# First feed-forward output by seven products for six block pairs, modulation spread over both mixers' outputs, last right-half products deferred

## The chip, the cores and the metric

The kernel runs on one NeuronCore of one Trainium2 chip. The time is microseconds on the device for one execution. TensorE is called PE in the profile, VectorE DVE, ScalarE ACT, GpSimd POOL and SyncE SP; each takes its instructions strictly in the order in which they stand in its queue, and the queues wait for each other by semaphores. Transfers between the device's memory and the on-chip buffers are issued by SP for the most part.

## What is computed

One step of a two-layer diffusion backbone over 640 tokens (512 latent, 128 context) of width 1024, in float32. Layer 0 mixes tokens by latent attention and neighbourhood attention, layer 1 by grouped-query attention; after each stands a SwiGLU feed-forward. Shift, scale and gate of every sub-layer come from a modulation vector; the two token groups have different ones.

```python
def ada_modulation(cond, w_mod, b_mod):
    m = jax.nn.silu(cond) @ w_mod + b_mod
    return jnp.split(m, 6, axis=-1)

def swiglu(h, w_in, w_out):
    gate, up = jnp.split(h @ w_in, 2, axis=-1)
    return (jax.nn.silu(gate) * up) @ w_out

for l in range(DEPTH):
    ...
    xs = xs + g1_s * out_s
    hs = modulate(rms_norm(xs, norm_ffn[l]), sh2_s, sc2_s)
    xs = xs + g2_s * swiglu(hs, w_ffn_in[l], w_ffn_out[l])
```

The hidden width of the feed-forward is 2816, which is 22 blocks of 128.

## The kernel before

Activations lie transposed: eight tiles `x[0]` to `x[7]` of 128 features by 640 tokens. A product works on a half of 320 tokens, left (c = 0) or right (c = 1); the right half holds 192 latent and 128 context tokens, so its evacuation with the gate (`residual`, L319 to L323) takes two DVE instructions where the left takes one. Every float32 factor is split into a high part, written by ACT, and a low part, written by DVE (in some places POOL) as the difference; a product of two split factors is three 128x320 products on PE (`mm3`, recorded at L63).

*Modulation.* The modulation of layer 0 for the first sub-layers is computed at the start. The remaining 56 tiles (eight for the gate G2 of layer 0, eight for each of the six parts of layer 1) are made on the side. One such tile is a load of 512 KB into `wm` and two DVE instructions `junk<-wm,cb`, which multiply it by the activated condition `cb` and sum along the row into `mods`. `mod_side` builds a function `step` that the feed-forward calls; its `plan` says how many tiles are fetched at which call. Before, 17 tiles were made in layer 0's feed-forward loop (one in each of the blocks 5 to 21), 11 in the first pass of its output, 20 in the second pass, and the last 8 in layer 1's loop.

*Mixer output* (`mixer_out`, tiles named `oa` in layer 0, `oc` in layer 1). Eight output tiles n. For n = 0 to 4 both halves are computed and evacuated at once; for 5, 6 and 7 the left halves come first, then PE runs `oanp` or `ocnp`, the product with ones that sums the squares for the norm of the left half, between right-half products of 5, 6, 7. The squares are made by ACT and added up by DVE into `oanacc` or `ocnacc` (L215), so the norm's product needs the last addition. The weights `oaw`, `ocw` of tile n are split by DVE for even n and by POOL for odd n (L185). After the norm, DVE makes the inputs of the feed-forward (`h01`, `h11`).

*Feed-forward* (`ffn`). A loop over the 22 hidden blocks computes gate and up by seven products for eight; the hidden blocks are split and most are spilled to memory. In layer 1 (`paired`), blocks 7 to 18 form six pairs (`PAIRS`); `split_pair` makes sums and differences of the two blocks and halves there (`T1` to `T4`, `B11`, `B21`, `B22`), so that the output product of a pair for two output tiles takes seven products instead of eight.

*Feed-forward output, first pass.* For each output tile n the blocks in `FIRST` (nine in layer 0, ten in layer 1) are multiplied, evacuated, and written back to `x[n]`. *Second pass.* In layer 0 the remaining 13 blocks are multiplied plainly, in 8 output tiles (names `fo_1_na`), with the last two tiles' right halves held back until the norm of the left half is under way. In layer 1 the second pass goes by pairs of output tiles p = 0 to 3 with seven products each, in the order S2, A11, S3, A12, A22, S1, S4 (`PLAN`): the weights S1, S2, S3, S4 are sums and differences of the raw blocks A11, A12, A21, A22, made by DVE (L1675 to L1685) and split at L1692 and L1693 three places ahead of their use. Their raw loads go through a ring of three buffers, tag `raw`, which the modulation tiles of the feed-forward's output use too.

## Time and profile before

Three runs took 1478.83, 1478.95 and 1480.19 us; the median is 1478.95. The profiled execution took 1480.2 us, of which the span from the first to the last instruction is 1478.4.

| stage | from, us | to, us |
|---|---|---|
| layer 0 mixer output (`oa`) | 303 | 377 |
| layer 0 feed-forward loop | 413 | 653 |
| layer 0 output, first pass | 654 | 717 |
| layer 0 output, second pass | 717 | 808 |
| layer 1 attention | 808 | 973 |
| layer 1 mixer output (`oc`) | 973 | 1045 |
| layer 1 feed-forward loop | 1082 | 1321 |
| layer 1 output, first pass | 1321 | 1391 |
| layer 1 output, second pass | 1391 | 1466 |
| last norm and stores | 1466 | 1478 |

A row of the timeline gives start, duration, engine, line, operation, output tile and input tiles, shape, and in brackets how long the engine was idle ahead of it and what released it. The name of a tile is its program name without buffer numbers. A row of busy time by stretch gives, for each engine, busy microseconds and the number of instructions, then the TensorE clock that was granted (1.00 is full), the DMA engines' share and the rate in GB/s.

### The profile page before, as it was taken

How to read it: one execution, taken by the hardware profiler on the slowest of the kernel's cores; microseconds unless marked ns; L12 is line 12 of the kernel's file. 1: busy time of each engine (PE TensorE's matmuls, PEld its weight loads, DVE VectorE, ACT ScalarE, POOL GpSimd, SP SyncE). 2: the span in 40 equal slices, each digit the busy share in tenths (PEclk: the TensorE clock that was granted, in tenths of full speed). 3: DMA queues.
4: the chain of work that ended last, by engine and by line, in shares of the span. 5: the costliest groups of instructions: out<-in, count | busy, mean ns of one | idle time of the engine just before them, and what ended most of it. 6: DMA issues, size and time to landing. Idle time of an engine off the chain costs nothing.

```text
span 1478.4 us, 25725 instructions
## 1 busy us (share of the span) xinstructions
PE 1440.5 (97%) x9785; PEld 1391.9 (94%) x9785; DVE 1202.6 (81%) x2236; ACT 769.9 (52%) x1521; POOL 210.9 (14%) x302
## 2 busy tenths in 40 slices
PE   5999999999999999999999999999999999999997
...
DVE  5686688876989999967997888766999999954496
...
GB/s 372 219 152 142 178 67 37 29 55 189 30 204 190 189 184 182 168 229 336 271 217 114 95 55 31 29 44 123 29 196 169 190 197 209 207 224 303 196 86 72
DMA packets 80651, 229.53 MB, mean 155 GB/s; under 512 B 9136, under 2 KB 14736, under 8 KB 80144
## 3 DMA queue, kind: packets, MB, share of 16 engines
...
## 4 chain that ended last, share of the span: by engine, by line
PE 85%; DVE 6%; ACT 4%; DMA 2%; issue 2%; SPq 0%; POOL 0%; DVEq 0%; ACTq 0%; POOLq 0%
PE fg L63 21%; PE fd L63 10%; PE fo L63 8%; PE fu L63 6%; PE gq L63 3%; DMA mraw<-in_wm 2%; PE nk L63 2%; PE nq L63 2%; PE fo_2b L63 1%; PE fo_0b L63 1%; PE gs L63 1%; PE fo_2a L63 1%; PE fo_0a L63 1%; PE go L63 1%; PE fo_4b L63 1%
## 5 line engine op out<-in xcount | busy, mean ns | idle before, releaser
L1805 DVE SCALAR_TENSOR_TENSOR junk<-wm,cb 128x1024 bf16<-128x1024 f32 x62 | 75.7, 1221 | 5.4 <-DMA wm<-in_wm 4.7
L1248 ACT ACTIVATE sg<-g 128x320 f32<-128x320 f32 x34 | 16.0, 472 | 115.0 <-DVE g L1248 115.0
L63 PE MATMUL gq<-h10h,wgq 128*128 128x320 f32 x256 | 66.7, 318 | 0.0
L255 POOL TENSOR_SCALAR h10h<-h10t,gs,mods 128x320 fp32r<-128x320 f32 x4 | 3.6, 888 | 429.5 <-DVE h10t L249 427.8
L1248 DVE SCALAR_TENSOR_TENSOR junk<-wm,cb 128x1024 bf16<-128x1024 f32 x50 | 61.1, 1221 | 0.8
L1248 DVE TENSOR_TENSOR wY<-s,wY 128x1024 fp32r<-128x1024 f32 x40 | 48.8, 1220 | 2.2 <-ACT wY L1248 2.2
L1248 DVE TENSOR_TENSOR wZ<-s,wZ 128x1024 fp32r<-128x1024 f32 x40 | 48.8, 1220 | 0.0
L63 PEld LDWEIGHTS gq<-h10h,wgq 128*128 128x128 f32 x256 | 45.0, 188 | 0.9 <-PE gtp L67 0.2
L1248 ACT ACTIVATE wZ<-s 128x1024 fp32r<-128x1024 f32 x40 | 42.4, 1060 | 0.1
L1248 ACT ACTIVATE wY<-s 128x1024 fp32r<-128x1024 f32 x40 | 42.0, 1049 | 0.0
L63 PE MATMUL gq<-h10l,wgq 128*128 128x320 f32 x128 | 39.5, 308 | 0.0
L1987 ACT ACTIVATE gp<-gs,gb,rq 128x640 f32<-128x640 f32 (+1 forms) x40 | 31.9, 797 | 14.5 <-DVE gb L1986 14.1
L63 PE MATMUL fg<-h11E,wW 128*128 128x320 f32 x240 | 38.7, 310 | 0.0
L63 PE MATMUL fg<-h11q,wX 128*128 128x320 f32 x240 | 38.6, 309 | 0.0
L63 PE MATMUL fg<-h01q,wX 128*128 128x320 f32 x240 | 38.6, 309 | 0.0
L63 PE MATMUL fg<-h11N,wZ 128*128 128x320 f32 x240 | 38.6, 309 | 0.0
L63 PE MATMUL fg<-h01N,wZ 128*128 128x320 f32 x240 | 38.6, 309 | 0.0
L63 PE MATMUL fu<-h01q,wX 128*128 128x320 f32 x240 | 38.6, 309 | 0.0
L63 PE MATMUL fu<-h11q,wX 128*128 128x320 f32 x240 | 38.6, 309 | 0.0
L63 PE MATMUL fg<-h01E,wW 128*128 128x320 f32 x240 | 38.6, 309 | 0.0
L63 PE MATMUL fd<-h11q,wZ 128*128 128x320 f32 x240 | 38.5, 309 | 0.0
L63 PE MATMUL fd<-h01q,wZ 128*128 128x320 f32 x240 | 38.5, 309 | 0.0
...
## 6 DMA issues: line engine op xcount, KB each, us to landing
wm<-in_wm SPq DMA_DIRECT2D x48, 512.0 KB, 4.0
mraw<-in_wm SPq DMA_DIRECT2D x8, 1024.0 KB, 15.4
mraw<-in_wm SPq DMA_DIRECT2D x16, 512.0 KB, 3.9
...
mrow<-in_wm0g POOLq DMA_DIRECT2D x8, 512.0 KB, 6.4
wm<-in_wm0g SPq DMA_DIRECT2D x8, 512.0 KB, 3.5
...
```

Of the source, the lines that this page charges most:

```text
L63: cls.last = nc.tensor.matmul(*a, **k)
L255: G.tensor_scalar(h[:, c0:c1], t, self.gsl[:, k, 0:1], self.ml[:, self.sh + k, 0:1], ALU.mult, ALU.add)
L1248: self.last = after(self.last, lambda: op(*a, **k))
L1805: def step(kind, at, line=lambda op, *a, **k: op(*a, **k)):
L1987: weighed.append((S.activation(dst, src, AF.Exp, bias=nb, scale=rq[:, j:j + 1], accum_out=ll[:, j:j + 1]), v))
```

## The change

Four things change together.

1. *Layer 0's output goes as layer 1's.* `FO_ORDER` is one list for both layers, `FIRST` has ten blocks in both, `split_pair` runs in layer 0's loop too, and the second pass has seven products for each of four pairs of output tiles.
2. *The second pass has a new order*, for both layers. `PLAN` is now a list of (p, product): for p = 0 and 1 S2, A11, S1, S4, S3, A12, A22; for p = 2 and 3 the left half's products S2, A11, S3, A12, A22; and at the end S1 and S4 of 2 and of 3. The norm of the left half is taken after A22 of p = 3, and the next layer's left inputs (or the final scaling) are made beside the deferred right-half products.
3. *Modulation is spread over both mixers' outputs.* There is one list `left` of 56 tiles; 8 are made in `oa` (1, 2, 2, 2, 1 at n = 0 to 4), 12 in layer 0's loop, 18 in the first pass of its output (1, 2, 2, 2, 2, 3, 3, 3), none in the second pass, 10 in `oc` (two at each n), 8 in layer 1's loop. In the mixers the tiles use a ring of two buffers, in the first pass the `raw` ring of three.
4. `cb` is loaded from the already activated condition `crs`, so its four activations and the input `crow` go.

```diff
-FO_ORDER = (TAIL + list(range(FB - 3)), TAIL + list(range(7)) + list(range(7, FB - 3, 2)) + list(range(8, FB - 3, 2)))
+FO_ORDER = TAIL + list(range(7)) + list(range(7, FB - 3, 2)) + list(range(8, FB - 3, 2))
...
-    def mixer_out(wsrc, os_, order, xin, ml, name, nxt, pre, begun, behind):
+    def mixer_out(wsrc, os_, order, xin, ml, name, nxt, pre, begun, behind, step):
...
                                 evac(i, c, ps[c])
+                            step("o", i)
                         held = []
...
                         evac(n, c, ps[c])
+                    step("o", n)
...
-        paired = l == 1
-        nf = 10 if paired else 9
-        FIRST, SECOND = FO_ORDER[l][:nf], FO_ORDER[l][nf:]
+        FIRST = FO_ORDER[:10]
...
-            PLAN = ("S2", "T2", "b"), ("A11", "B11", "a"), ("S3", "T3", "b"), ("A12", "B21", "a"), ("A22", "T4", "b"), \
-                ("S1", "T1", "c"), ("S4", "B22", "d")
+        KIND = {"S2": ("T2", "b"), "A11": ("B11", "a"), "S3": ("T3", "b"), "A12": ("B21", "a"), "A22": ("T4", "b"),
+                "S1": ("T1", "c"), "S4": ("B22", "d")}
+        LEFT, RIGHT = ("S2", "A11", "S3", "A12", "A22"), ("S1", "S4")
+        PLAN = [(p, c) for p in (0, 1) for c in LEFT[:2] + RIGHT + LEFT[2:]] + [(p, c) for p in (2, 3) for c in LEFT] + \
+            [(p, c) for p in (2, 3) for c in RIGHT]
...
+            if late and c in RIGHT:
+                if l == 1:
+                    scale_final(x, 1, n + 1 if c == "S1" else n)
+                nxt(x, nrm, 0, [next(order), next(order)])
...
-    def mod_side(todo, plan):
+    left = [(l, src[i], j0, i) for l, src, j0 in [(0, wm0g[:8], G2)] + [(1, wm1[j:j + 8], j) for j in (SH1, SC1, G1, SH2, SC2, G2)]
+            for i in range(8)]
+
+    def mod_side(plan):
...
+                    if raws is None:
+                        raw = load(src, D, f"wm{l}_{j0 + i}")
+                    else:
+                        raw = raws.tile([P, D], F32, tag="ws", bufs=2, name=f"wm{l}_{j0 + i}")
+                        nc.sync.dma_start(raw, src)
...
-    x, pend = mixer_out(wOA, oMs + oNs, [4, 5, 6, 7, 0, 1, 2, 3], x_again, mods[0], "oa", nxt, op[-1], begun, scored)
+    x, pend = mixer_out(wOA, oMs + oNs, [4, 5, 6, 7, 0, 1, 2, 3], x_again, mods[0], "oa", nxt, op[-1], begun, scored,
+                        mod_side(lambda kind, i: (1, 2, 2, 2, 1)[i])(op[1], op[5]))
...
-    side = mod_side([(0, wm0g[:8], G2)] + [(1, wm1[j:j + 8], j) for j in (SH1, SC1, G1, SH2, SC2)],
-                    lambda kind, i: int(i > 4) if kind == "fb" else (0, 1, 1, 1, 2, 2, 2, 2, 3, 3, 3, 3, 2, 2, 2, 2)[i])
+    side = mod_side(lambda kind, i: int(i in (5, 6, 7, 8, 10, 12, 14, 16, 18, 19, 20, 21)) if kind == "fb" else
+                    (1, 2, 2, 2, 2, 3, 3, 3)[i])
...
-    x, pend = mixer_out(wOC, oGs, list(range(8)), lambda n, x=x: x[n], mods[1], "oc", nxt, op[-1], begun, None)
+    x, pend = mixer_out(wOC, oGs, list(range(8)), lambda n, x=x: x[n], mods[1], "oc", nxt, op[-1], begun, None,
+                        mod_side(lambda kind, i: (2, 2, 2, 2, 2)[i])(op[1], op[5]))
```

Where the instructions stand now is seen best in DVE's queue. The first place is the start of `oc`, layer 1's mixer output: `xr` and `lead` are the residual tiles, `oc0a` and so on the sums in PSUM, `ocnsq` the squares, `ocw` the weights of the mixer's output. Before:

```order
L323 SCALAR_TENSOR_TENSOR xr_4323<-oc0a,mods_99,xr_4323 128x320
L323 SCALAR_TENSOR_TENSOR xr_4323<-oc0b,mods_99,xr_4323 128x192
L323 SCALAR_TENSOR_TENSOR xr_4323<-oc0b,mods_99,xr_4323 128x128
L323 SCALAR_TENSOR_TENSOR xr_4337<-oc1a,mods_99,xr_4337 128x320
L323 SCALAR_TENSOR_TENSOR xr_4337<-oc1b,mods_99,xr_4337 128x192
L323 SCALAR_TENSOR_TENSOR xr_4337<-oc1b,mods_99,xr_4337 128x128
L215 TENSOR_TENSOR ocnacc<-ocnacc,ocnsq_12077 128x320
L185 TENSOR_TENSOR ocw_12220<-ocw4r,ocw_12220 128x1024
L215 TENSOR_TENSOR ocnacc<-ocnacc,ocnsq_12085 128x320
L323 SCALAR_TENSOR_TENSOR xr_4383<-oc2a,mods_99,xr_4383 128x320
```

In the kernel after the change, from the same evacuation of `oc0a` on:

```order
L323 SCALAR_TENSOR_TENSOR lead_5330<-oc0a,mods_99,lead_5330 128x320
L323 SCALAR_TENSOR_TENSOR lead_5330<-oc0b,mods_99,lead_5330 128x192
L323 SCALAR_TENSOR_TENSOR lead_5330<-oc0b,mods_99,lead_5330 128x128
L1792 SCALAR_TENSOR_TENSOR junk_12227,mods_99<-wm_30_12223,cb 128x1024
L323 SCALAR_TENSOR_TENSOR xr_4344<-oc1a,mods_99,xr_4344 128x320
L1792 SCALAR_TENSOR_TENSOR junk_12229,mods_99<-wm_30_12223,cb 128x1024
L215 TENSOR_TENSOR ocnacc<-ocnacc,ocnsq_12240 128x320
L1792 SCALAR_TENSOR_TENSOR junk_12231,mods_99<-wm_31_12225,cb 128x1024
L323 SCALAR_TENSOR_TENSOR xr_4344<-oc1b,mods_99,xr_4344 128x192
L1792 SCALAR_TENSOR_TENSOR junk_12233,mods_99<-wm_31_12225,cb 128x1024
L323 SCALAR_TENSOR_TENSOR xr_4344<-oc1b,mods_99,xr_4344 128x128
```

The twenty `junk` instructions stand between the evacuations and additions from here on, the last one ahead of the addition for n = 5; the split of `ocw4r`, which was the eighth of these rows, has moved behind the fourteenth `junk`:

```order
L1792 SCALAR_TENSOR_TENSOR junk_12407,mods_99<-wm_36_12403,cb 128x1024
L215 TENSOR_TENSOR ocnacc<-ocnacc,ocnsq_12400 128x320
L1792 SCALAR_TENSOR_TENSOR junk_12409,mods_99<-wm_36_12403,cb 128x1024
L185 TENSOR_TENSOR ocw_12419<-ocw4r,ocw_12419 128x1024
L1792 SCALAR_TENSOR_TENSOR junk_12411,mods_99<-wm_37_12405,cb 128x1024
L323 SCALAR_TENSOR_TENSOR xr_4634<-oc5a,mods_99,xr_4634 128x320
L1792 SCALAR_TENSOR_TENSOR junk_12413,mods_99<-wm_37_12405,cb 128x1024
L185 TENSOR_TENSOR ocw_12532<-ocw6r,ocw_12532 128x1024
L323 SCALAR_TENSOR_TENSOR xr_4560<-oc4a,mods_99,xr_4560 128x320
```

The evacuation of `oc5a` and the split of `ocw6r` now stand ahead of that of `oc4a`.

The second place is DVE's queue at the end of layer 0's first pass (`fo_0_71` is the right half of its last output tile) and the start of its second. After the change:

```order
L1792 SCALAR_TENSOR_TENSOR junk_8813,mods_99<-wm_27_8805,cb 128x1024
L323 SCALAR_TENSOR_TENSOR xr_4710<-fo_0_71_8733,mods_98,xr_4710 128x192
L323 SCALAR_TENSOR_TENSOR xr_4710<-fo_0_71_8733,mods_98,xr_4710 128x128
L1792 SCALAR_TENSOR_TENSOR junk_8815,mods_99<-wm_28_8807,cb 128x1024
L1792 SCALAR_TENSOR_TENSOR junk_8817,mods_99<-wm_28_8807,cb 128x1024
L1792 SCALAR_TENSOR_TENSOR junk_8819,mods_99<-wm_29_8809,cb 128x1024
L1669 TENSOR_TENSOR wo_1_0S_8834<-wo_1_1A21r,wo_1_1A22r 128x768
L1792 SCALAR_TENSOR_TENSOR junk_8821,mods_99<-wm_29_8809,cb 128x1024
L1670 TENSOR_TENSOR wo_1_0S_8835<-wo_1_0S_8834,wo_1_0A11r 128x768
L1691 TENSOR_TENSOR wo_1_0A_8841<-wo_1_0A11r,wo_1_0A_8841 128x768
L1672 TENSOR_TENSOR wo_1_1A21r<-wo_1_0A11r,wo_1_1A21r 128x768
L1691 TENSOR_TENSOR wo_1_0S_8838<-wo_1_0S_8835,wo_1_0S_8838 128x768
```

For comparison the same engine at the same place of layer 1 in the kernel before, where such weights were made already:

```order
L1598 TENSOR_TENSOR wo_0_75_16283<-wo_0_75r,wo_0_75_16283 128x640
L1675 TENSOR_TENSOR wo_1_0S_16373<-wo_1_1A21r,wo_1_1A22r 128x768
L1676 TENSOR_TENSOR wo_1_0S_16374<-wo_1_0S_16373,wo_1_0A11r 128x768
L1678 TENSOR_TENSOR wo_1_1A21r<-wo_1_0A11r,wo_1_1A21r 128x768
L323 SCALAR_TENSOR_TENSOR xr_4622<-fo_0_6a,mods_99,xr_4622 128x320
L1693 TENSOR_TENSOR wo_1_0S_16377<-wo_1_0S_16374,wo_1_0S_16377 128x768
L1693 TENSOR_TENSOR wo_1_0S_16384<-wo_1_1A21r,wo_1_0S_16384 128x768
L323 SCALAR_TENSOR_TENSOR xr_4622<-fo_0_6b,mods_99,xr_4622 128x192
L323 SCALAR_TENSOR_TENSOR xr_4622<-fo_0_6b,mods_99,xr_4622 128x128
L1693 TENSOR_TENSOR wo_1_0A_16380<-wo_1_0A11r,wo_1_0A_16380 128x768
L1681 TENSOR_TENSOR wo_1_0S_16374<-wo_1_0A12r,wo_1_0S_16374 128x768
```

There the sums and splits of `wo_1_0S` stood ahead of the last evacuations of the first pass; in layer 0 of the changed kernel they stand behind the evacuation of `fo_0_71` and among four `junk` instructions.

The third place is the end of a pair of output tiles in layer 1's second pass: the evacuation of p = 0's left half, the additions after A22 (L1748) and the splits of p = 1's S2 (`wo_1_1S_16743`) and S1. After the change:

```order
L215 TENSOR_TENSOR fn1acc<-fn1acc,fn1sq_16768 128x320
L1669 TENSOR_TENSOR wo_1_2S_16739<-wo_1_3A21r,wo_1_3A22r 128x768
L323 SCALAR_TENSOR_TENSOR lead_13211<-fo_1_0a,mods_99,lead_13211 128x320
L1670 TENSOR_TENSOR wo_1_2S_16740<-wo_1_2S_16739,wo_1_2A11r 128x768
L1691 TENSOR_TENSOR wo_1_1A_16771<-wo_1_2A11r,wo_1_1A_16771 128x768
L1748 TENSOR_TENSOR fo_1_0p_16639<-fo_1_0b,fo_1_0p_16639 128x320
L1691 TENSOR_TENSOR wo_1_1S_16743<-wo_1_2S_16740,wo_1_1S_16743 128x768
L1691 TENSOR_TENSOR wo_1_1S_16794<-wo_1_2S_16739,wo_1_1S_16794 128x768
L323 SCALAR_TENSOR_TENSOR xr_4344<-fo_1_0p_16639,mods_99,xr_4344 128x320
```

The split of S2 for the next pair now stands behind the addition that needs A22's product, which is the last product of the pair.

## The prediction

> **What bounds the kernel now.** I read the page first: the busy table, the row of slices and the chain that ended last.

> ```profile
> span 1478.4 us, 25725 instructions
> PE 1440.5 (97%) x9785; PEld 1391.9 (94%) x9785; DVE 1202.6 (81%) x2236; ACT 769.9 (52%) x1521; POOL 210.9 (14%) x302
> PE   5999999999999999999999999999999999999997
> DVE  5686688876989999967997888766999999954496
> PE 85%; DVE 6%; ACT 4%; DMA 2%; issue 2%; SPq 0%; POOL 0%; DVEq 0%; ACTq 0%; POOLq 0%
> ```

> TensorE (PE) is busy in every slice but the first and the last, and the chain runs through it for 85% of the span. So the time is the number of products times their pitch, plus whatever makes PE wait. VectorE (DVE) has 19% free on the whole, but its slices differ: nines in the feed-forward loops, fours and sixes elsewhere. The second view is busy time by stage, with the two mixer stretches on which the argument rests.

> ```profile
> core 0: us, PE busy (x) PEld busy (x) DVE busy (x) ACT busy (x) POOL busy (x), PEclk, DMA share, GB/s
> 413.00:653.00 240.00, 240.00 (x1638) 239.81 (x1637) 223.11 (x325) 120.34 (x198) 0.00 (x0) 1.00 0.56 183
> 653.00:718.00 65.00, 65.00 (x446) 65.00 (x445) 49.97 (x90) 12.19 (x16) 0.00 (x0) 1.00 0.91 327
> 1391.00:1466.00 75.00, 75.00 (x511) 74.57 (x509) 56.84 (x98) 37.04 (x63) 0.00 (x0) 1.00 0.32 110
> 333.20:367.29 34.09, 34.09 (x235) 34.09 (x234) 22.36 (x33) 13.51 (x21) 10.53 (x4) 1.00 0.58 198
> 1001.05:1035.69 34.64, 34.64 (x238) 34.64 (x237) 22.88 (x33) 13.62 (x21) 9.93 (x4) 1.00 0.42 132
> ```

> PE never stops in these stretches. Its pitch is 65.00/446 = 145.7 ns to 75.00/511 = 146.8 ns for one 128x320 product, which is what a product taken away is worth here. DVE has about 12 us free in each mixer stretch.

> **What goes.** Layer 0's first output ran 1056 products; with ten blocks plain (480) and six pairs by seven products (4 x 7 x 18 = 504) it runs 984. The gain is 72 x 0.1465 = **10.5 us**, certain, since PE is full there. Everything else in the change can only give that back: it moves DVE work to places where PE waits for DVE. The unit moved is one modulation tile: one 512 KB load and two DVE products.

> ```profile
> 649.92 1.22 DVE L1248 SCALAR_TENSOR_TENSOR junk<-wm,cb 128x1024 bf16<-128x1024 f32 x1
> 651.07 0.08 DVE L1248 DVE_READ_ACCUMULATOR junk<-wm,cb 128x1 f32 x1
> wm<-in_wm SPq DMA_DIRECT2D x48, 512.0 KB, 4.0
> ```

> One product lasts 1.22 us and holds the queue 1.15 us (649.92 to 651.07); a load lands 4.0 us after its issue.

> **Second mixer (oc): the wait that decides most.** Ten tiles, twenty products, now stand in DVE's queue between the first evacuation of oc and the last addition to its norm, for which PE's ocnp waits in order.

> ```profile
> 1001.05 0.55 DVE L323 SCALAR_TENSOR_TENSOR xr<-oc0a,mods,xr 128x320 f32<-128x320 f32 x1 [5.85 <-PE oc0a L63]
> 1001.52 0.67 DVE L323 SCALAR_TENSOR_TENSOR xr<-oc0b,mods,xr 128x192 f32<-128x192 f32 x2
> 1002.10 0.54 DVE L323 SCALAR_TENSOR_TENSOR xr<-oc1a,mods,xr 128x320 f32<-128x320 f32 x1
> ...
> 1005.31 1.21 DVE L185 TENSOR_TENSOR ocw<-ocw4r,ocw 128x1024 fp32r<-128x1024 f32 x1
> 1006.45 0.48 DVE L215 TENSOR_TENSOR ocnacc<-ocnacc,ocnsq 128x320 f32<-128x320 f32 x1
> 1006.85 0.54 DVE L323 SCALAR_TENSOR_TENSOR xr<-oc2a,mods,xr 128x320 f32<-128x320 f32 x1
> ...
> 1010.86 2.44 DVE L215 TENSOR_TENSOR ocnacc<-ocnacc,ocnsq 128x320 f32<-128x320 f32 x1 [0.78 <-ACT ocnsq L214]
> ...
> 1035.20 0.49 DVE L215 TENSOR_TENSOR ocnacc<-ocnacc,ocnsq 128x320 f32<-128x320 f32 x1 [0.60 <-ACT ocnsq L214]
> 1036.49 0.70 PE L63 MATMUL ocnp<-ocnacc,ones 128*128 128x320 f32 x2
> ```

> The first row starts when PE releases it, so nothing can be done earlier. The queue from there, by starts: 8 left evacuations at 0.47, 5 right ones at 0.58, 11 additions at 0.40, 4 weight splits at 1.14 and three small rows, together 15.9, plus 20 x 1.15 = 23.0: 38.9 us. It ends at 1039.95 at the earliest, against 1035.69. PE would arrive at 1036.49, and 0.44 later because three more right-half products stand ahead, so at least 1039.95 - 1036.93 = 3.0 us are lost (3.8 if the 0.8 from the last addition to ocnp is needed too). Before, some additions were stretched (2.44 instead of 0.48 at 1010.86). By the busy time as it was, 22.88 + 20 x 1.22 = 47.3 us from 1001.05 end at 1048.3, a loss of 11.4. A split of GpSimd's lies under each stretched row, as in the first mixer:

> ```profile
> 342.16 2.42 POOL L185 TENSOR_TENSOR oaw<-oaw5r,oaw 128x1024 fp32r<-128x1024 f32 x1 [5.49 <-ACT oaw L184]
> 342.47 2.45 DVE L215 TENSOR_TENSOR oanacc<-oanacc,oansq 128x320 f32<-128x320 f32 x1 [0.77 <-ACT oansq L214]
> ```

> I expect about half of that stretching to stay: **7 us**, bounds 3.0 and 11.4. [...]

> **First mixer (oa).** Eight tiles, sixteen products.

> ```profile
> 329.24 0.58 DVE L1831 COPY xr<-oMs3l 128x1 f32<-128x1 f32 x8
> 333.20 0.55 DVE L323 SCALAR_TENSOR_TENSOR xr<-oa0a,mods,xr 128x320 f32<-128x320 f32 x1 [3.38 <-PE oa0b L63]
> ...
> 366.80 0.49 DVE L215 TENSOR_TENSOR oanacc<-oanacc,oansq 128x320 f32<-128x320 f32 x1 [0.59 <-ACT oansq L214]
> 368.10 0.70 PE L63 MATMUL oanp<-oanacc,ones 128*128 128x320 f32 x2
> ```

> A product now stands ahead of the first evacuation, so part of the 3.38 us idle serves. Unstretched, 15.7 + 16 x 1.15 = 34.1 us from 329.82 end at 363.9: no loss. By the busy time as it was, 329.82 + 22.36 + 19.5 = 371.7, a loss of 3.6; two buffers for the tiles, with 4.0 us to land, can add 2 more. **3 us**, bounds 0 and 5.6.

> **Start of layer 0's second pass.** In layer 1 of the kernel before, the same weights are made like this:

> ```profile
> 1378.90 0.96 DVE L1675 TENSOR_TENSOR wo_0S<-wo_1A21r,wo_1A22r 128x768 f32<-128x768 f32 x1 [3.22 <-DMA wo_1A22r<-in_wFO]
> 1379.89 0.96 DVE L1676 TENSOR_TENSOR wo_0S<-wo_0S,wo_0A11r 128x768 f32<-128x768 f32 x1
> 1380.88 0.85 ACT L1692 ACTIVATE wo_0S<-wo_0S 128x768 fp32r<-128x768 f32 x1 [6.07 <-DVE wo_0S L1676]
> 1382.10 0.95 DVE L1693 TENSOR_TENSOR wo_0S<-wo_0S,wo_0S 128x768 fp32r<-128x768 f32 x1
> ...
> 1391.67 0.68 DVE L323 SCALAR_TENSOR_TENSOR xr<-fo,mods,xr 128x192 f32<-128x192 f32 x2 [1.65 <-PE fo L63]
> ...
> 1391.47 1.78 PE L63 MATMUL fo_0b<-hr_T,wo_0S 128*128 128x320 f32 x11
> ```

> S2 is split by 1383.05, eight microseconds before PE needs it, and the last evacuation of the first pass comes after. In layer 0 now DVE's queue has that evacuation first, which PE releases only at the pass's end, and behind it three modulation products, the sum S1, a fourth product, S2, the split of A11, a difference and then S2's low half. Counted from PE's last product of the pass: 0.68 + 3 x 1.22 + 0.96 + 1.22 + 0.96 = 7.5, ScalarE's high half 0.85 gives 8.3, and DVE's three rows of 0.95, less an overlap of 0.08 each, give 10.1 for the low half. PE has six products (0.9) to do in between. A11's raw load waits for a buffer that the second product frees and 4.0 us to land, 0.68 + 2.44 + 4.0 = 7.1 against the 6.5 at which S2 could begin: 0.6 more, or 1.4 on a busy queue. **9.5 us**, bounds 8.3 and 11.5, with nothing to hide it: PE's queue is in order.

> **The rest.** Layer 0's first pass gets 18 tiles instead of 11, beside ten blocks of weights: DVE 71.5 us of work by row pitches in about 69 of PE, and 27.5 to 29 MB in that time, some 400 GB/s against the 327 in the row above: 0 to 4, I take 1.2. In both second passes A22 is the last left product, and its row stands ahead of the next pair's S2 split; in layer 1 before, the split ended as follows,

> ```profile
> 1407.61 0.95 DVE L1693 TENSOR_TENSOR wo_1S<-wo_2S,wo_1S 128x768 fp32r<-128x768 f32 x1
> ```

> 1.4 us before the next pair could start (1391.47 + 7 x 18 x 0.1468 = 1409.97), so waits of up to an addition and a split appear at some of three transitions in each layer: 0.3 to 1.5 in each, I take 0.6 and 0.6. Layer 0 also gets a norm product (0.35) and the next layer's left inputs start later in DVE's queue: 0.2 to 2, I take 1.6. At the tail two additions more on the chain, 0.8 by the 0.40 above, less what the earlier left half saves: 0.4. The feed-forward loop of layer 0 loses five tiles (12.2 us of DVE) and gains the operand sums (18.5): about 229 of its 240 us, so one tight block, 0.3, at most 0.7.

> **The clock.** Long waits have a second price here.

> ```profile
> 201.19 0.42 PE L63 MATMUL ns<-nk,nqh 128*128 128x384 f32 x1 [1.05 <-DVE kTl L865]
> 201.90:205.30 3.40, 3.40 (x15) 3.40 (x14) 2.89 (x11) 2.20 (x6) 0.37 (x1) 0.50 0.49 130
> 8.00:12.00 4.00, 0.00 (x0) 0.00 (x0) 3.93 (x13) 3.96 (x11) 0.00 (x0) 1.00 1.03 397
> ```

> After waits of about 1 us, 3.4 us ran at half the granted clock, which is 1.7 us lost; after an empty stretch at 8 to 12 us none did. Three new long waits therefore cost 0 to 5.1; I take 1.7, one window. [...]

> **Sum.** 3 + 7 + 9.5 + 1.2 + 1.2 + 1.6 + 0.4 + 0.3 + 1.7 = 25.9 given back, less 10.5: +15.4 on the profiled execution's 1480.2, which stands 1.25 above the median 1478.95. On the median: **1494**. The bounds add to 12.5 (1481.0) and 44.1 (1512.5).

> **Rivals.**
> *Nothing is stretched.* If GpSimd's splits hold no DVE row up once the queue is packed, oa costs 0 and oc 3.0, no window is halved, and the terms lie at their lower ends: 12.5 - 10.5 = +2.0, 1481.0, within 0.2% of before (1476 to 1482). It decides at the additions: all at 0.49 instead of the 2.44 above. For it: the products leave GpSimd fewer gaps. Against: four splits of 2.4 us are still there. 0.15.
> *The gain stays.* If DVE's queue did not stand between PE and its next weights at the second pass, and the mixers' slack of 12 us covered the twenty products, only 10.5 less some small terms would be seen: 1470 to 1475. It needs DVE to overtake its own queue; 0.05.
> *Saturation.* DMA at 0.91 in the first pass already, now with seven more tiles of 512 KB: if loads land late there, and all three waits halve the clock, 4 + 5.1 instead of 1.2 + 1.7: +21.6, and with oc at its upper end +26.5: 1500 to 1506 and more. 0.17.

> **Numbers.** Forecast 0.63, rivals 0.15, 0.05, 0.17. A measurement of this kernel tells about 0.2% (3 us) from no change. Faster 0.06 (the second rival and a little), same 0.14, slower 0.80. The range 1479 to 1508 leaves out the second rival and the far end of the third.

> **What would show it.** Right: PE idle for 8 to 11 us ahead of layer 0's first S2 product, with S2's low half as releaser; ocnp 4 to 12 us later after its predecessor than before, with the vector engine full from oc0a on; oanp 0 to 6. The first output of layer 0 shows 984 products. Wrong: no gap at the second pass's start, which would mean that S2 was split before the evacuation; or ocnp reached with DVE idle ahead of it.

## The result and the profile after

The changed kernel takes **1515.55 us** (median of 4 runs, 1512.87 to 1518.16); the kernel before, run beside it, takes 1479.57 (4 runs, 1478.83 to 1480.28). The ratio is **1.024, 95% interval 1.0228 to 1.0252**: slower by 36 us. The profiled execution took 1513.64 us with a span of 1511.9, which is 33.5 us more than the span of before. All lengths below are of profiled executions. A wait of PE is given as the time from one product to the next, less one pitch of 0.147 us; the idle time in the bracket of a row is up to 0.3 us shorter.

From the page of the kernel after: the span, the busy table, the slices of PE and of its clock, and the engines' shares of the chain that ended last.

```profile
span 1511.9 us, 25918 instructions
PE 1444.9 (96%) x9715; PEld 1389.6 (92%) x9715; DVE 1255.4 (83%) x2345; ACT 788.0 (52%) x1573; POOL 213.5 (14%) x302
PE   6999999998999999999799999998999999999996
PEclk9999999999999999999899999998999999999998
PE 72%; DVE 14%; DMA 6%; ACT 5%; issue 3%; SPq 0%; DVEq 0%; POOL 0%; ACTq 0%; POOLq 0%
```

PE issues 70 products fewer (72 taken away, 2 for a second norm row), yet its busy time rises by 4.4 us: some of them ran slower. Two slices that were full now show a dip in PE and in the clock, near 740 and near 1040 us; a third, near 360, shows one in PE alone. The chain says who took the time: DVE had 6% of it and has 14%, DMA had 2% and has 6%.

Cut at the same landmarks on PE, the 33.5 us lie as follows (stage lengths, before and after):

| from ... to (on PE) | before | after | difference |
|---|---|---|---|
| start ... first product of oa | 303.12 | 301.73 | -1.4 |
| oa ... oanp, the first mixer's norm | 64.98 | 72.18 | +7.2 |
| oanp ... layer 0's first output product | 282.73 | 284.46 | +1.7 |
| layer 0's output, to its last product | 156.94 | 160.37 | +3.4 (-10.5 of products in it) |
| ... attention's first `gr`, the norm of the queries | 28.46 | 32.67 | +4.2 |
| ... ocnp, the second mixer's norm | 200.26 | 214.52 | +14.3 |
| ocnp ... layer 1's first output product | 282.75 | 284.44 | +1.7 |
| layer 1's output, to the end | 159.15 | 161.49 | +2.3 |

The second mixer first. The windows of the kernel after (columns: length, busy time and count of PE, PEld, DVE, ACT, POOL, then granted clock, DMA share, GB/s) from the first evacuation to the last addition of each mixer's norm, and its rows on VectorE, on GpSimd and on PE:

```profile
331.32:373.85 42.53, 36.08 (x243) 35.29 (x241) 40.85 (x66) 13.88 (x21) 12.55 (x4) 0.98 0.74 254
...
1016.32:1065.88 49.56, 40.34 (x246) 38.72 (x244) 47.25 (x76) 13.59 (x21) 11.83 (x4) 0.89 0.57 188
```

```profile
1018.98 2.97 DVE L1792 SCALAR_TENSOR_TENSOR junk<-wm,cb 128x1024 bf16<-128x1024 f32 x1
...
1026.40 1.23 DVE L1792 SCALAR_TENSOR_TENSOR junk<-wm,cb 128x1024 bf16<-128x1024 f32 x1 [1.08 <-DMA wm<-in_wm]
...
1027.56 2.69 DVE L215 TENSOR_TENSOR ocnacc<-ocnacc,ocnsq 128x320 f32<-128x320 f32 x1
...
1053.65 3.22 DVE L1792 SCALAR_TENSOR_TENSOR junk<-wm,cb 128x1024 bf16<-128x1024 f32 x1
...
1056.81 3.41 DVE L185 TENSOR_TENSOR wgu<-wgu_0r,wgu 128x1024 fp32r<-128x1024 f32 x1
...
1065.39 0.49 DVE L215 TENSOR_TENSOR ocnacc<-ocnacc,ocnsq 128x320 f32<-128x320 f32 x1 [0.59 <-ACT ocnsq L214]
```

```profile
1017.90 2.96 POOL L185 TENSOR_TENSOR ocw<-ocw3r,ocw 128x1024 fp32r<-128x1024 f32 x1 [18.71 <-ACT ocw L184]
1026.77 3.13 POOL L185 TENSOR_TENSOR ocw<-ocw5r,ocw 128x1024 fp32r<-128x1024 f32 x1 [5.91 <-ACT ocw L184]
1053.38 2.40 POOL L185 TENSOR_TENSOR ocw<-ocw7r,ocw 128x1024 fp32r<-128x1024 f32 x1 [23.48 <-ACT ocw L184]
1055.75 3.39 POOL L185 TENSOR_TENSOR wgu<-wgu_1r,wgu 128x1024 fp32r<-128x1024 f32 x1
```

```profile
1035.28 0.60 PE L63 MATMUL oc4b<-oGs0h,ocw 128*128 128x320 f32 x1 [2.75 <-DVE xr L323]
...
1038.43 0.61 PE L63 MATMUL oc5a<-oGs0h,ocw 128*128 128x320 f32 x1 [2.28 <-DVE xr L323]
...
1065.93 1.43 PE L63 MATMUL ocnp<-ocnacc,ones 128*128 128x320 f32 x2 [3.52 <-DVE ocnacc L215]
```

VectorE is busy for 47.25 of 49.56 us where it was busy for 22.88 of 34.64: the queue is the stage now. Each of GpSimd's four splits meets a row of VectorE that takes 2.7 to 3.4 us in place of 0.48 or 1.22. Read the first pair together: the split ends at 1017.90 + 2.96 = 1020.86, the product at 1018.98 + 2.97 = 1021.95, so the product does its own 1.1 us after the split has ended. It is the same in the others (1029.90 and 1030.25, with an addition of 0.4; 1055.78 and 1056.87; 1059.14 and 1060.22). The other way round, the three splits here that started beside a running product took longer, by about that product's remainder: 2.96, 3.13 and 3.39 us in place of 2.40, beside remainders of 0.7, 0.9 and 1.1 (the one at 1055.75 beside the row that ends at 1056.87). The four overruns of VectorE's rows are 1.75 + 2.2 + 2.0 + 2.2 = 8.2 us. And PE waits not only at ocnp (3.7 us), but twice before it (2.9 and 2.6), for banks that late evacuations free.

The start of layer 0's second pass, on VectorE, ScalarE and PE of the kernel after:

```profile
732.27 0.67 DVE L323 SCALAR_TENSOR_TENSOR xr<-fo,mods,xr 128x192 f32<-128x192 f32 x2
...
736.54 0.95 DVE L1669 TENSOR_TENSOR wo_0S<-wo_1A21r,wo_1A22r 128x768 f32<-128x768 f32 x1
...
738.73 0.96 DVE L1670 TENSOR_TENSOR wo_0S<-wo_0S,wo_0A11r 128x768 f32<-128x768 f32 x1
```

```profile
739.72 1.58 ACT L1690 ACTIVATE wo_0S<-wo_0S 128x768 fp32r<-128x768 f32 x2
```

```profile
740.62 0.90 PE L63 MATMUL fo_0b<-hr_T,wo_0S 128*128 128x320 f32 x2 [9.64 <-ACT wo_0S L1690]
```

PE's previous product started at 730.66. Behind the last evacuation stand three products, S1, one more product and S2, as forecast, and PE finds its weights 9.8 us late.

Four windows of the kernel after show the clock (columns as above): behind oanp, at the start of the second pass, inside oc, and behind ocnp.

```profile
375.40:378.87 3.47, 3.47 (x14) 3.47 (x14) 2.43 (x6) 2.88 (x6) 0.53 (x2) 0.50 0.15 58
740.62:744.11 3.49, 3.49 (x12) 3.31 (x13) 3.49 (x5) 1.52 (x2) 0.00 (x0) 0.50 0.98 346
...
1038.43:1045.70 7.27, 7.02 (x28) 6.76 (x29) 7.27 (x14) 0.82 (x2) 0.00 (x0) 0.59 0.51 155
1067.40:1071.70 4.30, 4.30 (x18) 4.30 (x18) 3.24 (x7) 3.29 (x6) 1.33 (x2) 0.50 0.03 10
```

Each stretch follows a wait of PE. Against products at 0.1467 us they cost 1.56, 1.74, 3.29 and 1.92: **8.5 us** together, where before had one such stretch ahead of its tail, at 203 us, of 1.15 by the same count. The sum is good to about 1 us: the last 1.1 us of the third window ran at full clock, and the two norm products, 1.43 us each in place of 0.70, stand ahead of the first and the last window.

### The profile page after: what moved, and what is told of

Same layout as the page of the kernel before. It is cut to its first block, busy times and chain, and to the rows that moved or that the text cites. A ratio compares the mean times of both kernels' runs of the same rounds, so it can differ in the third digit from the quotient of the medians.

```text
span 1511.9 us, 25918 instructions
## 1 busy us (share of the span) xinstructions
PE 1444.9 (96%) x9715; PEld 1389.6 (92%) x9715; DVE 1255.4 (83%) x2345; ACT 788.0 (52%) x1573; POOL 213.5 (14%) x302
## 3 DMA queue, kind: packets, MB, share of 16 engines
q8 instruction: 76, 1.25, 0.3%
## 4 chain that ended last, share of the span: by engine, by line
PE 72%; DVE 14%; DMA 6%; ACT 5%; issue 3%; SPq 0%; DVEq 0%; POOL 0%; ACTq 0%; POOLq 0%
PE fg L63 21%; PE fd L63 9%; PE fu L63 7%; DVE junk L1792 4%; PE fo L63 3%; PE gq L63 3%; DMA wm<-in_wm 2%; PE nk L63 2%; PE nq L63 2%; PE fo_0b L63 1%; PE gs L63 1%; DMA mraw<-in_wm 1%; DVE xr L323 1%; PE go L63 1%; PE fo_0a L63 1%
## 5 line engine op out<-in xcount | busy, mean ns | idle before, releaser
L1792 DVE SCALAR_TENSOR_TENSOR junk<-wm,cb 128x1024 bf16<-128x1024 f32 x72 | 96.3, 1337 | 11.6 <-DMA wm<-in_wm 8.4
L63 PE MATMUL gq<-h10h,wgq 128*128 128x320 f32 x256 | 66.7, 318 | 0.0
L1248 ACT ACTIVATE sg<-g 128x320 f32<-128x320 f32 x28 | 13.2, 472 | 90.8 <-DVE g L1248 90.8
L1248 DVE TENSOR_TENSOR wY<-s,wY 128x1024 fp32r<-128x1024 f32 x40 | 48.7, 1218 | 2.2 <-ACT wY L1248 2.2
L1248 DVE SCALAR_TENSOR_TENSOR junk<-wm,cb 128x1024 bf16<-128x1024 f32 x40 | 48.8, 1221 | 0.7
L1248 DVE TENSOR_TENSOR wZ<-s,wZ 128x1024 fp32r<-128x1024 f32 x40 | 48.7, 1218 | 0.0
L63 PEld LDWEIGHTS gq<-h10h,wgq 128*128 128x128 f32 x256 | 45.0, 188 | 1.0 <-PE gtp L67 0.2
L1248 ACT ACTIVATE wZ<-s 128x1024 fp32r<-128x1024 f32 x40 | 42.4, 1060 | 0.1
L1248 ACT ACTIVATE wY<-s 128x1024 fp32r<-128x1024 f32 x40 | 42.0, 1049 | 0.0
L63 PE MATMUL gq<-h10l,wgq 128*128 128x320 f32 x128 | 39.4, 308 | 0.0
L63 PE MATMUL fg<-h01q,wX 128*128 128x320 f32 x240 | 38.8, 309 | 0.0
L63 PE MATMUL fu<-h01q,wX 128*128 128x320 f32 x240 | 38.7, 309 | 0.0
L63 PE MATMUL fg<-h11E,wW 128*128 128x320 f32 x240 | 38.7, 310 | 0.0
L63 PE MATMUL fg<-h11q,wX 128*128 128x320 f32 x240 | 38.6, 309 | 0.0
L63 PE MATMUL fg<-h01N,wZ 128*128 128x320 f32 x240 | 38.6, 309 | 0.0
L63 PE MATMUL fg<-h11N,wZ 128*128 128x320 f32 x240 | 38.6, 309 | 0.0
L63 PE MATMUL fu<-h11q,wX 128*128 128x320 f32 x240 | 38.6, 309 | 0.0
L63 PE MATMUL fg<-h01E,wW 128*128 128x320 f32 x240 | 38.6, 309 | 0.0
L63 PE MATMUL fd<-h11q,wZ 128*128 128x320 f32 x240 | 38.5, 309 | 0.0
L63 PE MATMUL fd<-h01q,wZ 128*128 128x320 f32 x240 | 38.5, 309 | 0.0
## 6 DMA issues: line engine op xcount, KB each, us to landing
wm<-in_wm SPq DMA_DIRECT2D x48, 512.0 KB, 3.9
mraw<-in_wm SPq DMA_DIRECT2D x16, 512.0 KB, 4.0
mrow<-in_wm0g POOLq DMA_DIRECT2D x8, 512.0 KB, 6.5
wm<-in_wm0g SPq DMA_DIRECT2D x8, 512.0 KB, 4.9
```

The costliest lines, as they stand in the source:

```text
L63: cls.last = nc.tensor.matmul(*a, **k)
L1248: self.last = after(self.last, lambda: op(*a, **k))
L1792: def step(kind, at, line=lambda op, *a, **k: op(*a, **k)):
```

## The experiments

Theory: the change loses its gain because VectorE's queue, in order, stands between PE and what PE needs, at the two mixers and at the start of the second pass; GpSimd's splits lengthen that queue, and each wait is paid again at half clock. The rivals are named with each experiment. Medians of four runs unless said otherwise, ratios with 95% intervals to the kernel before on the same chip, whose median was 1480.26 to 1480.88. The changed kernel was not run again beside them, so a difference from its 1515.55 carries about 1 us more.

**Tiles of one stage made almost free.** The products of one stage read 32 of 1024 columns; the loads, the waits for them and the order stay.

```diff
-    def mod_side(plan):
+    def mod_side(plan, width=D):
...
-  line(V.scalar_tensor_tensor, junk, raw, 1.0, cb[:, c, :], ...
+  line(V.scalar_tensor_tensor, junk[:, :width], raw[:, :width], 1.0, cb[:, c, :width], ...
...
-  mod_side(lambda kind, i: (2, 2, 2, 2, 2)[i])(op[1], op[5]))
+  mod_side(lambda kind, i: (2, 2, 2, 2, 2)[i], 32)(op[1], op[5]))
```

In oc alone:

> The kernel after the change, but in the second mixer's output (oc) each of the twenty modulation products covers 32 of 1024 columns (the tiles are loaded as before; ten modulation columns of layer 1 come out wrong). Theory (the products fill VectorE's queue ahead of the norm's last addition): the distance from the first oc evacuation to ocnp falls from 49.6 us to about 36, the three waits in oc (2.9, 2.6 and 3.7 us) and the half clock behind them go, about 15.5 us in all, 1500 us (1498 to 1503). Rival (the tiles' loads or the changed order of the weights hold the stage up): at most half of that, 1507 or more.

Measured 1503.78 (1500.92 to 1506.0), ratio 1.0156 (1.0141 to 1.0171), 0.8 us above the range expected. The stage up to ocnp falls from +14.3 to +3.5, what follows it from +2.3 to +0.1. So most of the loss there is the length of the queue, and the half clock goes with it. What is left shows on VectorE and PE of this run:

```profile
1018.29 2.43 DVE L1792 SCALAR_TENSOR_TENSOR junk<-wm,cb 128x32 bf16<-128x32 f32 x1
...
1024.31 0.19 DVE L1792 SCALAR_TENSOR_TENSOR junk<-wm,cb 128x32 bf16<-128x32 f32 x1 [0.28 <-DMA wm<-in_wm]
...
1028.11 0.51 DVE L1792 SCALAR_TENSOR_TENSOR junk<-wm,cb 128x32 bf16<-128x32 f32 x1 [2.96 <-DMA wm<-in_wm]
```

```profile
1048.88 0.41 PE L63 MATMUL oc<-oGs0h,ocw 128*128 128x320 f32 x1 [2.48 <-POOL ocw L185]
```

A product of 0.19 us took 2.43 beside a split of GpSimd's (1018.25 to 1020.67); the tiles' two buffers make the queue wait for loads, up to 2.96 us; and PE waits for a split that was late.

In oa alone:

> The same in the first mixer's output (oa): sixteen products cover 32 of 1024 columns (G2 of layer 0 comes out wrong). Theory: the waits of 1.5 and 5.2 us go and the half clock behind them (1.6), 8.3 us, 1507 us (1505 to 1509). Rival (the changed order of loads in front of oa, with the condition and the first tile ahead of the residual tiles): the first evacuations stay late and less than 4 us go, 1511 or more.

Measured 1509.92 (1507.76 to 1512.64), ratio 1.02 (1.0184 to 1.0216): oa's +7.2 becomes +0.7, and the +2.4 behind oanp +0.1. The median is 0.9 above the range expected: the two stages give back 8.8 us in the profiled execution, but layer 0's output, which the edit leaves as it is, takes 2.4 more there.

In layer 0's first pass alone:

> The kernel after the change, but the 36 modulation products of layer 0's first pass cover 32 of 1024 columns (all tiles are loaded as before; eighteen modulation columns of layer 1 come out wrong). Theory (VectorE's queue sets the wait at the second pass's start): the products leave it, the evacuation, the sum, S2 and its split stay, so the wait falls from 9.8 us to 3.5 to 5.5; the first pass has no waits; with less half clock 1509 us (1507 to 1511). Rival (the raw weights come late through the ring of three buffers): the wait stays above 8 us, 1514 or more.

Measured 1509.01 (1506.67 to 1511.23), ratio 1.0191 (1.0176 to 1.0206), as expected. The wait at the second pass's start falls from 9.8 to 4.0 us, but a new one of 2.6 opens at the first change of pairs, and half clock costs 2.7 instead of 1.7 there. That last difference is not the edit's: e1 and e2, with the wait of 9.8 unchanged, ran at half clock there for 5.4 and 5.1 us in place of 3.5. In the profiled execution 3.0 us of the gain lie in layer 0's output; 2.5 lie in and behind oa, ahead of the edit, where executions differ among themselves.

In all three:

> All modulation products of both mixers' outputs and of layer 0's first pass cover 32 of 1024 columns; all tiles are loaded. The three terms are separate in time, so they should add: about 8.5 for oa, 12 for oc (as measured with that part alone) and 6 for the first pass, 1489 us (1486 to 1492). That is still above the kernel before: if the products alone were the loss it would be 1469, so what is left (some 20 us above that) belongs to loads that come late through the rings, to GpSimd's stretching, to the second pass's order and to the next layer's inputs. Rival (the losses cover each other): less than 20 us gained, 1496 or more.

Measured 1493.15 (1491.01 to 1494.63), ratio 1.0083 (1.0068 to 1.0098), 1.2 us above the range expected. The three alone took off 11.8, 5.6 and 6.5 us, 23.9 in sum; together they take off 22.4. The stages add up nearly without one hiding another.

**The tiles left out.** The 36 tiles of both mixers and the first pass are neither loaded nor multiplied; the modulation columns they make are zero.

```diff
+                    if kind in none:
+                        held.append((l, j0, i, None))
+                        continue
...
+                    if raw is None:
+                        V.memset(mods[l][:, j0 + i, :], 0.0)
-                    for c in range(2):
+                    for c in range(2 if raw is not None else 0):
```

> The kernel after the change without the 36 modulation tiles of both mixers' outputs and of layer 0's first pass, neither loads nor products (their modulation columns are zero; a small write stands for each). What is left is the layer-0 output by seven products, the new order of the second pass and the rest. Theory (waits and half clock come from these tiles but for the transitions between pairs, about 3.7 us in layer 0 and 2.1 in layer 1, and the next layer's inputs, 4.2): 1479.5 - 10.5 + 10 = 1479 us (1475 to 1483), with no wait at the second pass's start. Rival (the second pass of layer 0 waits at its start whatever the tiles, since its weights stand behind the last evacuation): 4 us more and a half clock behind, 1485 or more.

Measured 1479.67 (10 runs, 1477.64 to 1484.35), ratio 0.9991 (0.9981 to 1.0001). So the tiles where they now stand cost 35.9 us, as much as the whole loss against before, which makes these tiles too, at other places. Their products are 22.4 us of that (e6); the other 13.5 go only when the loads go too, 8.7 of them in layer 0's output by the profiled executions of e6 and e10. How much of the 13.5 is late loads, how much short rows that GpSimd stretches and how much the order of the queue, no run separates. VectorE and PE at the second pass's start in this run:

```profile
713.95 0.96 DVE L1669 TENSOR_TENSOR wo_0S<-wo_1A21r,wo_1A22r 128x768 f32<-128x768 f32 x1 [4.67 <-DMA wo_1A22r<-in_wFO]
...
725.27 0.68 DVE L323 SCALAR_TENSOR_TENSOR xr<-fo,mods,xr 128x192 f32<-128x192 f32 x2 [1.65 <-PE fo L63]
```

```profile
725.07 2.80 PE L63 MATMUL fo_0b<-hr_T,wo_0S 128*128 128x320 f32 x18
...
745.50 0.68 PE L63 MATMUL fo_1b<-hr_T,wo_1S 128*128 128x320 f32 x2 [1.81 <-ACT wo_1S L1690]
```

S1 is made 11 us ahead of the last evacuation, as in layer 1 of the kernel before, and PE goes from one pass to the next without a gap. But the kernel is not faster than before either. In the profiled execution, the slowest of the ten (1484.35), the 10.5 us of products are spent again: 5.3 in layer 0's output (2.0 and 1.1 of waits at two changes of pairs and 1.6 at half clock behind the first are 4.7 of it), 4.1 from there to attention's first `gr`, and 2.9 from layer 1's first output product to the end. That is 12.3; another 2.1 lie ahead of oa.

**GpSimd's splits in both mixers taken away.** They become copies on ScalarE.

```diff
-  after(at[1], lambda: (V if lo == "v" else G).tensor_tensor(lw, raw, f(hi), ALU.subtract)))
+  after(at[1], lambda: S.activation(lw, raw, AF.Copy) if lo == "s" else (V if lo == "v" else G).tensor_tensor(...)))
...
-  lo="g" if n % 2 else "v"
+  lo="s" if n % 2 else "v"
...
-  w.append(unit(wFI[l, 0, i], 1024, f"wgu{l}_{i}", "vg"[i], pool=fp))
+  w.append(unit(wFI[l, 0, i], 1024, f"wgu{l}_{i}", "vs"[i], pool=fp))
```

> The kernel after the change, but GpSimd splits nothing in the two mixers' outputs: the low parts of the odd tiles' weights and of one feed-forward tile are a copy written by ScalarE instead of the difference written by GpSimd (those low parts are wrong). VectorE has the same rows in nearly the same order. Theory (each of GpSimd's four splits per mixer blocks one VectorE row for its whole length): the four stretched rows fall from 2.7 to 3.4 us to 0.5 to 1.2, 8.2 us in oc and 6.6 in oa leave the queue, and with the half clock behind the waits 12 to 17 us go, 1501 us (1498 to 1504). Rival (the stretched rows wait for their input or a load, and GpSimd is beside the point): they stay as long, no change beyond 3 us.

Measured 1494.38 (1493.84 to 1495.67), ratio 1.0093 (1.0076 to 1.011): 21 us off, more than expected. oa loses 0.2 us instead of 7.2. From its first product to the feed-forward loop, oc now loses 2.9 (+6.1 to ocnp, -3.2 behind it, since 22 more of oc's own products stand ahead of ocnp in this run); the three half-clock stretches in and behind the mixers are gone (mean granted clock 0.993, 0.984 after). On VectorE and PE at the end of oc:

```profile
1052.35 0.48 DVE L215 TENSOR_TENSOR ocnacc<-ocnacc,ocnsq 128x320 f32<-128x320 f32 x1
```

```profile
1053.04 0.70 PE L63 MATMUL ocnp<-ocnacc,ones 128*128 128x320 f32 x2
```

VectorE went from its first evacuation (1012.30) to that last addition in 40.5 us, where the prediction had 38.9 for the queue without any stretching, and PE did not stop at ocnp. So the prediction's lower bounds (0 and 3.0) were the mixers without GpSimd. The rest takes GpSimd's splits and the products together: with the products short and GpSimd in place (e1, e2), oc loses 3.5 and oa 0.7.

The same edit in the kernel before:

> The kernel before the change, with GpSimd's splits in both mixers' outputs replaced as in the experiment on the kernel after (the low parts are a copy written by ScalarE, so they are wrong). Theory (the stretched rows were there before, but inside VectorE's 12 us of free time): no change, 1479.5 us within 1.5. Rival (they already cost time): 3 us or more faster.

Measured 1480.74 (10 runs, 1479.49 to 1481.82), ratio 1.0002 (0.9993 to 1.0012). There the same stretching cost nothing that can be measured: VectorE had 12 us to spare in each stage. The same edit was worth 0 us with that queue and 21 with the full one.

The same splits given to VectorE, where they lie over no other row:

```diff
-  lo="g" if n % 2 else "v"
+  lo="v"
...
-  w.append(unit(wFI[l, 0, i], 1024, f"wgu{l}_{i}", "vg"[i], pool=fp))
+  w.append(unit(wFI[l, 0, i], 1024, f"wgu{l}_{i}", "v", pool=fp))
```

> The kernel after the change with GpSimd's splits in both mixers' outputs (the odd tiles' weights and one feed-forward tile) made by VectorE instead. The result is right. VectorE gets 4 x 1.14 = 4.6 us more in each mixer and loses the stretching (8.2 and 6.6). The splits stand behind modulation products in its queue now, so PE waits for weights at oc3 to oc5 and oa5. Theory (the stretching is worth more than the splits): 2 to 10 us faster, 1510 us (1505 to 1513). Rival (the later weights cost as much as is gained): 1514 or more.

Measured 1515.79 (1510.52 to 1520.06), ratio 1.0235 (1.0207 to 1.0263): no change, a miss; the rival holds. PE in oc of this run:

```profile
1034.80 0.39 PE L63 MATMUL oc4a<-oGs0h,ocw 128*128 128x320 f32 x1 [1.93 <-DVE xr L323]
...
1041.81 0.63 PE L63 MATMUL oc3a<-oGs0h,ocw 128*128 128x320 f32 x1 [2.86 <-DVE ocw L185]
```

The stretching is gone, but the splits now stand in the same full queue, behind products of tiles, and PE waits for weights as well as for evacuations.

**The tiles moved within the first pass**, none beside the last output tile:

```diff
-                    (1, 2, 2, 2, 2, 3, 3, 3)[i])
+                    (2, 2, 3, 3, 3, 3, 2, 0)[i])
```

> The kernel after the change with the 18 tiles of layer 0's first pass at 2, 2, 3, 3, 3, 3, 2, 0 instead of 1, 2, 2, 2, 2, 3, 3, 3. All modulation products now stand ahead of the pass's last evacuation in VectorE's queue, the sums and splits of S2 still behind it. Theory (the queue's rows between the evacuation and S2's low half are the wait): the four products (4.9 us) leave it, the wait at the second pass's start falls from 9.8 us to 4 to 5.5, the first pass itself gets up to 1 us of waits, 1510 us (1508 to 1513). Rival (the raw weights arrive late through the ring of three buffers, whatever the queue): the wait stays over 8 us, no change.

Measured 1518.16 (1516.66 to 1523.13), ratio 1.026 (1.0241 to 1.0279): a miss. It is no faster, and the interval overlaps that of the kernel after. The wait at the second pass's start does fall, from 9.8 to 3.7 + 0.8 us, so those products were some 5 us of it. But the work comes out elsewhere: waits of 2.8, 1.6 and 1.0 inside the pass and 2.6 at the first change of pairs; layer 0's output takes 4.8 us longer than in the kernel after. In neither of the two placings that were run did the pass have room for 18 tiles.

**Tiles spread over attention too**: 5 beside oa, 13 in layer 0's loop, 4 beside oc, and one in each of attention's 8 heads, which leaves seven buffers instead of eight for the attention weights.

```diff
-  mod_side(lambda kind, i: (1, 2, 2, 2, 1)[i])(op[1], op[5]))
+  mod_side(lambda kind, i: (1, 1, 1, 1, 1)[i])(op[1], op[5]))
...
-  side = mod_side(lambda kind, i: int(i in (5, 6, 7, 8, 10, 12, 14, 16, 18, 19, 20, 21)) if kind == "fb" else
+  side = mod_side(lambda kind, i: int(i in (5, 6, 7, 8, 10, 12, 14, 15, 16, 18, 19, 20, 21)) if kind == "fb" else
...
-  pt = gp.tile([P, T], F32, tag="gp", bufs=8, name=f"gp{h}_{j}")
+  pt = gp.tile([P, T], F32, tag="gp", bufs=7, name=f"gp{h}_{j}")
...
-  mod_side(lambda kind, i: (2, 2, 2, 2, 2)[i])(op[1], op[5]))
+  mod_side(lambda kind, i: (0, 1, 1, 1, 1)[i])(op[1], op[5]))
...
+        gside("h", h)
```

> The kernel after the change with the same 56 modulation tiles at other places: 5 instead of 8 in oa, 13 instead of 12 in layer 0's feed-forward loop, 4 instead of 10 in oc, and 8 in layer 1's attention, one at each head (scratch for them there in a general buffer, and one buffer of eight less for the attention weights). Theory (a mixer stage has about 12 us of VectorE free, and only what is above that is lost, with the half clock behind it): 7.3 us of products leave oa and 14.6 oc, the waits there nearly vanish, 7 and 14 us; attention has some 27 us free and takes 2 to 6 of them back, 1499 us (1494 to 1504). Rival (every tile costs its 2.4 us wherever it stands): attention takes back more than 10, 1508 or more.

Measured 1508.55 (1506.22 to 1511.02), ratio 1.0188 (1.0168 to 1.0208): between the two, nearer the rival. The mixers recover (oa +1.9, oc +6.9), but attention loses 6.6. Attention in the kernel after, and in this run:

```profile
851.50:988.70 137.20, 135.63 (x929) 129.51 (x927) 113.79 (x251) 93.10 (x215) 32.52 (x38) 1.00 0.13 41
```

```profile
847.50:991.20 143.70, 136.94 (x928) 129.43 (x927) 129.18 (x280) 92.54 (x215) 38.96 (x38) 1.00 0.20 68
```

VectorE had 23 us free there and got 15.4 more to do, and PE still stopped, for 6.8 us of the stretch in place of 1.6; one of these waits, 2.0 us ahead of the product at 872.61, is for ScalarE's `gqh`. That rows come late because the products stand ahead of them on VectorE is the likely reading, not a shown one: the run also took a buffer from the attention weights, and GpSimd's rows there grew from 32.5 to 39.0 us. Free time on the average of a stage is not free time in front of the row that PE waits for.

**The deferral undone for the third pair**, so that only the last pair's right products stand at the end:

```diff
-  PLAN = [(p, c) for p in (0, 1) for c in LEFT[:2] + RIGHT + LEFT[2:]] + [(p, c) for p in (2, 3) for c in LEFT] + \
-      [(p, c) for p in (2, 3) for c in RIGHT]
+  PLAN = [(p, c) for p in (0, 1, 2) for c in LEFT[:2] + RIGHT + LEFT[2:]] + \
+      [(3, c) for c in LEFT + RIGHT]
...
-            late = p > 1
+            late = p > 2
...
```

> The kernel after the change with the right half's products S1 and S4 of the pair p = 2 back in their place, only those of p = 3 at the end (both layers). Theory (the order of the second pass costs at the transitions between pairs, not by the deferral itself): in layer 1 the second pass from its first product to the end of the span changes by less than 1 us; in layer 0 the next layer's left inputs have fewer additions ahead of them in VectorE's queue, 1 to 3 us less between the last output product and attention; 1513 us (1511.5 to 1515). Rival (the deferral itself costs about 2 us in each layer): 4 us less, 1511 or lower, with 2 of them in layer 1.

Measured 1514.07 (1511.88 to 1517.25), ratio 1.0227 (1.021 to 1.0243). The deferral of the third pair is not the cost: layer 1 takes as long from its second pass to the end (89.43 us, 89.26 after), with one wait of 1.9 at a change of pairs instead of 0.92 and 1.14. The next layer's inputs do not come earlier (+4.7 in that stage), which was expected of it and is a miss.

**The long wait filled with work.** Sixty products that nobody reads stand in the gap ahead of the second pass; they write a bank that the next product overwrites.

```diff
+            fill = j == 0 and l == 0
...
+            if fill:
+                dh, dl = kept[FB - 1]
+                for i in range(60):
+                    PE.matmul(b[p][to][:, :HT], dh[:, 0:P], dh[:, 0:HT], start=True, stop=True)
```

> The kernel after the change with sixty additional 128x320 products (of tiles already there, into the bank that S2's first product then clears) between the first and the second pass of layer 0, where PE waits 9.8 us. They take 8.8 us. Theory (the half clock comes from the wait): the wait is filled, no half clock follows it, the stage from the first output product to the norm is 1.7 us shorter, 1514 us. Rival (the half clock has another cause): the half clock stays at about 740 us, and the time is the same or longer by what of the sixty products isn't hidden.

Measured 1517.42 (1512.53 to 1519.32), ratio 1.0237 (1.0214 to 1.026). PE at that place, and the window behind it:

```profile
737.17 8.96 PE L63 MATMUL fo_0b<-hd_0h 128*128 128x320 f32 x60
...
747.97 0.56 PE L63 MATMUL fo_0b<-hr_T,wo_0S 128*128 128x320 f32 x2 [0.57 <-ACT wo_0S L1690]
```

```profile
745.97:749.46 3.49, 2.06 (x13) 1.68 (x12) 3.38 (x4) 2.98 (x4) 0.00 (x0) 1.00 0.91 297
```

The clock stays at 1.00 where it was 0.50, so the half clock there did come of the gap. The time is no better: PE is waiting for weights in that window (2.06 us busy of 3.49, where VectorE is busy for 3.38; two idle times of its rows, 0.86 and 0.57, end with ScalarE's `wo_0A` and `wo_0S`), and runs on to the next row that is late. The 1.7 us that the faster clock was expected to bring were not gained.

Nothing tried beats the kernel before. With the tiles gone altogether the changed output only equals it (0.9991), so no other placing of the tiles was pointed to as a gain.

## Why the prediction failed in size

The direction was right, and every place that it named is a place of loss but for the first pass and the loop. The time lay 21.6 us above the forecast and 7.6 above the range. The bounds of the terms add up to +33.6, as much as was measured in the profiled executions; the range stated stopped short of them. Term by term, in the profiled executions:

| term | predicted (bounds) | measured |
|---|---|---|
| products gone | -10.5 | -10.5 |
| first mixer, oa | 3 (0 to 5.6) | 7.2 |
| second mixer, oc | 7 (3.0 to 11.4) | 11.0, its half clock apart |
| start of the second pass | 9.5 (8.3 to 11.5) | 9.8 |
| first pass | 1.2 (0 to 4) | none over 0.6 |
| changes of pairs, both layers | 0.6 + 0.6 | 1.4 + 2.1 |
| norm product and next inputs | 1.6 (0.2 to 2) | 4.4 |
| tail; loop | 0.4; 0.3 | 0.1; 0.0 |
| half clock | 1.7 (0 to 5.1) | 8.5 |

The rest of the 33.5 is -1.4 ahead of oa, -1.3 in the two loops' starts, and some 2.2 in smaller waits and between the listed stretches, of which 1.5 are the two norm products at half clock. These are one execution's numbers: in the runs that leave oa as it is (e1, e3, e5, e7, e8) it lost 5.0 to 8.1 us, and where oc is left as it is (e2, e3, e5, e7, e8) that lost 13.7 to 14.6, its half clock in it. The term that failed most is the **clock**, then oa, oc and the next inputs.

**The mixers.** The step that failed was "I expect about half of that stretching to stay". None went: all four splits in each mixer found a row of VectorE under them, 2.69 to 3.41 us long. With the queue full there was one there each time, and so the spare 12 us, in which a blocked row cost nothing (e11, 1.0002), was the only thing that had kept the price down. e1's product of 0.19 us, which took 2.43 beside a split of 2.42, shows the same. The prediction put the whole stretching of before at the upper bound and then took the middle. The queue behind the upper bound was too short as well, and in oa the loss of 7.2 passed that bound of 5.6. It took VectorE's busy time of before with the products on top, 47.3 us; the stage took 49.6, which is 38.9 unstretched, 8.2 stretched and 2.3 idle for a load and for ScalarE's squares. It had no idle time in it, and no account of GpSimd's side: its splits grew too (of the eight in both mixers two took over 2.5 us before, 2.72 and 3.27; after, six took 2.96 to 3.42), and in oa one of them came late itself:

```profile
362.76 0.42 PE L63 MATMUL oa<-oNs0h,oaw 128*128 128x320 f32 x1 [1.32 <-POOL oaw L185]
...
373.91 1.43 PE L63 MATMUL oanp<-oanacc,ones 128*128 128x320 f32 x2 [5.01 <-DVE oanacc L215]
```

The working of the unstretched queue was right: e4 took 40.5 us against 38.9, and lost 0.2 in oa and 2.9 in oc against 0 and 3.0.

**Second pass.** The order of the queue was right; that 9.5 came so near to 9.8 is partly luck. One product more than counted (1.2 us) stood ahead of the last evacuation, and the low half of S2 that it added to the chain (10.1 instead of 8.3) did not hold PE up, which had another operand's products to do meanwhile. What released PE was ScalarE's high half, not the low half that the prediction named as the sign. Rival "the gain stays" falls here: VectorE's rows came in the order of its queue, the last evacuation at 732.27, S1 at 736.54 and S2 at 738.73, with the four products between.

**First pass.** Right that it would be full: this run shows no wait over 0.6 in it, others one of 1.5 (e7) or 2.3 us (e12), with the same 18 tiles. Saturation of DMA, the third rival, is not the main thing: with all loads kept and only the products shortened (e6), 22 of the 35.9 us came back. At the second pass's start 4.0 us were left that way (e5), and they go with the loads (e10); whether it is the loads' time or the place that their buffers give the next weights in the queue is not shown.

**Next layer's inputs.** Sized at 1.6, it is 4.4. As many products, 211, stand between the last output product and attention's first `gr` before and after; 3.2 us of waits are new, and the rest are products spaced out by late inputs at full clock. VectorE of the kernel after:

```profile
813.27 0.49 DVE L1756 TENSOR_TENSOR fo_2k<-fo_2c,fo_2k 128x320 f32<-128x320 f32 x1 [0.51 <-PE fo_2c L63]
...
814.93 0.55 DVE L241 SCALAR_TENSOR_TENSOR h10t<-lead,gs,fn0rs 128x320 f32<-128x320 f32 x1
```

The first input row stands 5.1 us behind the norm product (809.82), 2.5 before, with additions of right-half products ahead of it. Over the two stages from that norm product on, VectorE has 36.0 us of rows where it had 31.9, and 4.1 is about what is lost. That is a reading and no proof: e7 moved half of those additions away and got nothing back, e10 shows +4.3 with no tile near. Which rows of the seven-product output cost it stays open.

**The clock.** The step that failed was "I take 1.7, one window": there were four stretches at half clock, 8.5 us. The waits were counted as three and came as five of over 2 us: two in oc ahead of ocnp were not foreseen, since the prediction looked for oc's wait only at the norm. Half clock followed all three waits that the prediction knew (5.2, 9.8 and 3.7 us, with 0.50 in the windows behind them), and shorter waits were paid here too: 2.9 and 2.6 in oc (0.59), and 2.0 at e10's change of pairs, the longest wait of that run between oa and its tail (clock 0.54 behind it). One window instead of three was taken because of the row at 8 us, read as an empty stretch that no half clock follows. That was a misreading: PE does no product in that row, and the clock record of the trace begins only at 17.55 us, so the 1.00 is no measurement. Groups of one kind of product of the kernel before, in the windows 15.5 to 17.2, 17.6 to 18.2 and 22.7 to 23.5 us (count, busy us, mean ns), show the clock behind the 7.9 us for which PE waited until 13.12:

```profile
L63 PE MATMUL mod<-mraw,scol 128*32 128x256 f32 x16 | 1.9, 634 | 0.0
...
L63 PE MATMUL mod<-mraw,scol 128*32 128x256 f32 x16 | 1.2, 416 | 0.0
...
L63 PE MATMUL mod<-mraw,scol 128*32 128x256 f32 x16 | 1.1, 385 | 1.4 <-DMA mraw<-in_wm 1.4
```

In the first window their groups of four start 0.41 to 0.43 us apart (15.55, 15.98, 16.41, 16.83), from 17.6 us on 0.21 (17.63, 17.84, 18.06): behind that long wait PE was slow too. Without the row at 8 us the prediction's own figure was the 5.1 for all three waits.
